# Gate, queries and keys in pairs of column tiles with seven products, and other work beside the values, in a hybrid mLSTM and attention block

## The chip, the cores and the metric

The kernel runs on one core of one Trainium2 chip. The metric is device time in microseconds (us) of one launch, the median of several runs. Everything is computed in fp32; a product of fp32 matrices is made of three TensorE passes over two-part operands (a rounded high part and the rest).

## The reference

One encoder block over 2048 tokens of width 1024. The change is in the first projection and what reads it:

```python
xn = rms_norm(x, g)                         # 2048 x 1024
proj = xn @ W_in                            # q | k | v | o | gates | c_q | c_kv | k_rope
qk = silu(dwconv3_centred(concat([q_pre, k_pre]), conv_w, conv_b))
h = h_fwd + h_bwd                           # chunkwise mLSTM, both directions, 4 heads x 128
y_A = sigmoid(o_pre) * rms_norm(h, norm_g)
q = rms_norm(c_q, q_norm_g) @ w_uq          # 4 heads x (128 + 64), the 64 with rope
kv = rms_norm(c_kv, kv_norm_g) @ w_ukv
h = x + concat([y_A, attention(q, kv, k_rope)]) @ W_out
```

After it come a gated MLP with a convolution and a per-layer input embedding, which the change leaves alone.

## The kernel before

The first projection (`in_proj`) holds all of x in SBUF as two-part operands: `xh[c][f]` and `xl[c][f]` for token quarter c (512 tokens) and half f of the 1024 inputs. It runs in four stages, each of which is a stream of matmuls on PE (the engine of matmuls; DVE, ACT and POOL are the vector, scalar and GpSimd engines, SP issues all DMAs). Each stage is long, and PE's order is that of the code.

The rest stage makes 464 columns (gates, latent queries and keys) for 16 token tiles. A tile of x comes turned from memory (512 KB, in pieces of 512 bytes), ACT casts its high part and DVE subtracts for the low one. Beside it `ssq_x` squares the tile on ACT, adds the eight blocks down to two on DVE (L232, L233) and lets PE sum over the partitions with matmuls against ones (`ssp`, L236); the reciprocal norm goes into `rcol`, and at the end into memory (`r_d`, L319, one DMA of 4-byte pieces).

The values (`OFF_V`, L324) and the output gate (`OFF_O`, L335) follow with 16 tiles of 24 matmuls each, 128 tokens by 512 columns; the mLSTM's gates, a generator, are computed a little at a time beside them. Then queries and keys: eight column tiles j of 128 columns by four token quarters c, transposed, each `block` of 24 matmuls, followed by the convolution over tokens (`conv`: ACT for the first tap, DVE for two more, silu on ACT). Between the matmuls a `pump` (L371) draws 0.986 steps of side work for each six matmuls. The side work is two generators: `absorb` multiplies parts of attention's weights into each other, head by head from `w_out` (`wor`, `woa`, `woo`), and `q_up` makes attention's queries in eight cycles of 256 tokens: load `qraw`, split it (`cq`), multiply, rotate on DVE (`qtt`, `qro`, `qsr`, L598 to L605), transpose, and write to `q_d`.

PE's order in this last stage is written out by hand; the other engines' rows follow from a scheduler that puts an instruction where it thinks it will be ready. Every engine works through its rows in order, SP its DMA issues too: a row that waits holds up all rows behind it on that engine. Working places are named: `x0` to `x15`, `w0` to `w13`, `t0` to `t7`, `u0` to `u2`; who takes a place waits until its last user is done.

The seven-product form exists already in the later MLP (`L1427`): a product of 2 x 2 blocks made of seven block products, with sums of blocks ahead of them and behind. A product there is 12 matmuls of 128 by 512.

Of the kernel before, what the change touches and what calls it, by code (L numbers as in the profile page):

```python
# [19 lines left out]
P = 128  # L20
# [40 lines left out]
class Block:  # L61
# [4 lines left out]
    def __init__(self, ctx, tc, d):  # L66
# [17 lines left out]
        self.o_d = dt([NT, P, 512], F32, name="o_d")  # L84
# [89 lines left out]

    def in_proj(self):
        nc, d = self.nc, self.d
        xh = [[self.at(f"x{4 * c + 2 * f}", [P, 4, 512], F32R, f"xh{c}{f}") for f in range(2)] for c in range(4)]
        xl = [[self.at(f"x{4 * c + 2 * f + 1}", [P, 4, 512], F32R, f"xl{c}{f}") for f in range(2)] for c in range(4)]
        wrot, rrot, trot, srot = _rot("w", (*range(9), 13)), _rot("w", range(9, 13)), _rot("t", range(4)), _rot("s", range(3))
        w_in = d["w_in"][0].rearrange("(a b p) c -> a p b c", b=2, p=P)  # L180

        def load_w(c0, n, before=None):
# [18 lines left out]
            for k2 in range(KT // 2):  # L201
                if k2 == len(raws):
                    load(k2)
                raw = raws[k2]
                for b in range(2):
                    w = self.at(next(wrot), [P, 2, 512], F32R, "wsp")
# [4 lines left out]
        def nat(st, ws, n):  # L211
            ps = self.bank()
            c, o = st // 4, (st % 4) * P
            for kt in range(KT):
                f, k = divmod(kt, 4)
                self.mm3(ps[:, :n], xh[c][f][:, k, o:o + P], xl[c][f][:, k, o:o + P],
                         ws[kt][:, 0, :n], ws[kt][:, 1, :n], kt == 0, kt == KT - 1)
            return ps
# [8 lines left out]
        def ssq_x(st, x_t):  # L227
# [5 lines left out]
            nc.vector.tensor_tensor(ss[:, 0:2], ss[:, 0:2], ss[:, 2:4], op=ALU.add)  # L233
            ps = self.pml.tile([P, 4], F32, name="ssp", tag="ml")
            for i in range(2):
                nc.tensor.matmul(ps, ss[:, i], ones, start=i == 0, stop=i == 1)  # L236
            t = self.stat(1, "rsm")
            nc.vector.tensor_scalar(t, ps[:, 0:1], 1.0 / D, EPS, op0=ALU.mult, op1=ALU.add)
            nc.gpsimd.tensor_tensor(rcol[:, st:st + 1], t, self.nhalf[:, :1], op=ALU.pow)
# [48 lines left out]
        ones = self.cst.tile([P, 4], F32, name="ones")  # L288
        nc.vector.memset(ones, 1.0)
        nq, xq = {}, {}  # L290
# [10 lines left out]
        ws = load_w(OFF_R, NREST, first)  # L301
        for st in range(NT + LAG_X):
            if st + 1 < NT:
                xq[st + 1] = load_x(st + 1)
            if st == 0:
# [4 lines left out]
            if 1 <= st < NT:  # L310
                split_x(st, xq[st])
            if 0 <= st - 1 < NT:
                ssq_x(st - 1, xq.pop(st - 1))
# [6 lines left out]
        gates = self.gates()  # L320

        ws = load_w(OFF_V, 512)
        for st in range(NT):
            ps = nat(st, ws, 512)  # L324
            if st < LAG_R:
                turn_rest(NT - LAG_R + st, nq.pop(NT - LAG_R + st))
            t = self.at(next(trot), [P, 512], name="vo")
            nc.vector.tensor_scalar(t, ps, rcol[:, st:st + 1], None, op0=ALU.mult)
            nc.sync.dma_start(self.v_d[st], t)
            if st >= LAG_R:  # L330
                next(gates, None)

        ws = load_w(OFF_O, 512)
        go = self.row_bcast(self.at("t6", [P, 512], name="go"), d["mlstm_norm_g"][0], 512)
        for st in range(NT):  # L335
            ps = nat(st, ws, 512)
            t = self.at(next(trot), [P, 512], name="vo")
            nc.scalar.activation(t, ps, AF.Sigmoid, scale=rcol[:, st:st + 1])
            nc.vector.tensor_tensor(t, t, go, op=ALU.mult)
            nc.sync.dma_start(self.o_d[st], t)  # L340
            next(gates, None)
        for _ in gates:
            pass

        cw = self.at("w13", [32, P], name="cw")
        nc.sync.dma_start(cw[0:24], d["conv_qk_w"][0].rearrange("t (j p) -> (t j) p", p=P))
        nc.sync.dma_start(cw[24:32], d["conv_qk_b"][0].rearrange("(j p) -> j p", p=P))
        pc = self.tbank([P, 32])
        nc.tensor.transpose(pc, cw, self.ident[:32, :32])
        cwt = self.cst.tile([P, 4, 8], F32, name="cwt")  # L350
        nc.vector.tensor_copy(cwt.rearrange("p a b -> p (a b)"), pc)
        H = S // 2
        side = chain(self.absorb(), self.q_up())
        urot, wrot = _rot("u", (0, 1, 2)), _rot("w", (6, 9, 10, 11))

        def load_qk(j):
            raw = self.at("w12", [P, KT, P], name="wraw")
            nc.sync.dma_start(raw, d["w_in"][0, :, j * P:(j + 1) * P].rearrange("(k p) c -> p k c", p=P))
            out = []
            for f in range(2):  # L360
                w = self.at(next(wrot), [P, 4, 2, P], F32R, "wqk")
# [1578 lines left out]
```

## Time and profile before

| | us |
|---|---|
| median of 3 runs | 2960.42 (2960.11 to 2964.19) |
| profiled execution, span | 2960.1 |
| PE busy | 2893.7 |
| DVE busy | 1991.1 |
| ACT busy | 1477.1 |
| DMA, share of 16 engines | 52.1% |

The median is of whole runs, and the span is that of the profiled execution from its first to its last instruction. Busy time is what an engine spent in its own instructions; a window is a stretch of the span, for which the same is counted. "Idle before, releaser" names what ended an engine's wait. A matmul's own duration in the lists is longer than its pace, since matmuls are pipelined; the pace is the distance between starts.

### The profile page before, as it was taken

What the parts mean: (1) busy time and instruction counts of PE and PEld (TensorE: products, weight loads), DVE (VectorE), ACT (ScalarE), POOL (GpSimd) and SP (SyncE); (2) the same over time, 40 slices, a digit from 0 to 9 for tenths busy, and PEclk for the clock granted to TensorE, in tenths of its full rate; (3) what the DMA queues carried; (4) which work ended last, traced back from release to release, by engine and by line L of the source; (5) the groups of instructions that cost most, each with busy time, mean ns of one, the idle gap of its engine ahead of it and who ended that gap; (6) DMA issues with size and microseconds to landing.
All of it is one profiled execution on the core that took longest, in us unless ns stands there. A gap on an engine that the chain in (4) does not pass through costs nothing.

```text
span 2960.1 us, 40997 instructions
## 1 busy us (share of the span) xinstructions
PE 2893.7 (98%) x14750; PEld 2436.9 (82%) x14750; DVE 1991.1 (67%) x3679; ACT 1477.1 (50%) x2887; POOL 146.5 (5%) x279
## 2 busy tenths in 40 slices
PE   8999999999999999999999999999999999999998
PEld 7888888888888888788788888788887788878776
DVE  7522555777777777635677877767777767676776
ACT  7311544656665666523455555655556333244754
POOL 3100000000000000000000000000000000001111
PEclk9999999999999999999999999999999999999999
DMA  6512444443333343457734544657776657575854
GB/s 193 121 61 92 146 132 153 121 144 99 103 99 101 97 121 114 145 179 262 237 136 168 191 165 152 207 175 236 231 235 194 225 189 241 168 252 197 286 190 157
DMA packets 396540, 496.93 MB, mean 168 GB/s; under 512 B 32416, under 2 KB 265904, under 8 KB 396336
## 3 DMA queue, kind: packets, MB, share of 16 engines
q1 hardware_dynamic: 396336, 494.31, 52.1%
q8 instruction: 116, 1.90, 0.3%
q14 instruction: 88, 0.72, 0.1%
HBM read 318.39 MB, written 175.83 MB: 167 GB/s over the span
## 4 chain that ended last, share of the span: by engine, by line
PE 46%; DVE 4%; DMA 4%; issue 2%; ACT 2%; POOL 0%; SPq 0%; POOLq 0%; ACTq 0%; DVEq 0%
PE fxy L1427 29%; PE fz L1427 12%; PE bk L131 4%; PE fs L131 1%; DMA opr<-t_d 1%; DMA opr<-tw_d 1%; DVE op L121 1%; DVE fw L121 1%; DMA tsum<-x_d 0%; ACT fw L118 0%; DVE pj L1773 0%; ACT junk L1787 0%; DMA h_d<-fh 0%; ACT op L118 0%; PE tb L1075 0%
## 5 line engine op out<-in xcount | busy, mean ns | idle before, releaser
L1427 PE MATMUL fxy<-op,fw 128*128 128x512 f32 x3552 | 854.4, 392 | 18.1 <-DVE fh L1413 5.8
L1427 PEld LDWEIGHTS fxy<-op,fw 128*128 128x128 f32 x3552 | 660.7, 188 | 175.9 <-ACT ug L1584 13.9
L1427 PE MATMUL fz<-op,fw 128*128 128x512 f32 x1776 | 441.0, 391 | 6.5 <-DVE xt L1143 3.3
L1427 PEld LDWEIGHTS fz<-op,fw 128*128 128x128 f32 x1776 | 332.6, 188 | 76.1 <-DVE xt L1143 3.6
L118 ACT CAST pt<-tb 128x512 fp32r<-128x512 f32 x256 | 147.2, 586 | 176.7 <-PE tb L972 176.0
L131 PE MATMUL bk<-wsp,xh 128*128 128x512 f32 (+1 forms) x768 | 234.0, 385 | 0.0
L914 DVE TENSOR_REDUCE mx<-bk 128x1 f32<-128x512 f32 x256 | 175.0, 685 | 69.9 <-PE bk L913 65.1
L1427 PE MATMUL fxy<-op,fwd 128*128 128x512 f32 (+1 forms) x888 | 214.4, 390 | 0.9 <-ACT gate L1768 0.8
L131 PE MATMUL ppv<-pt,kv 128*128 128x256 f32 x1536 | 203.9, 287 | 0.0
L121 DVE TENSOR_TENSOR pt<-tb,pt 128x512 fp32r<-128x512 f32 x256 | 174.0, 684 | 37.5 <-ACT pt L118 36.5
L1427 PEld LDWEIGHTS fxy<-op,fwd 128*128 128x128 f32 x888 | 165.7, 188 | 35.9 <-ACT gate L1768 1.2
L932 ACT ACTIVATE pe<-bk,nm 128x512 f32<-128x512 f32 x256 | 174.6, 696 | 31.3 <-DVE nm L926 27.1
L131 PEld LDWEIGHTS ppv<-pt,kv 128*128 128x128 f32 x1536 | 188.9, 191 | 0.5 <-ACT pt L118 0.4
L131 PE MATMUL bk<-wo,yhl 128*128 128x512 f32 x744 | 176.2, 395 | 5.5 <-DVE yhl L121 5.5
L131 PEld LDWEIGHTS bk<-wo,yhl 128*128 128x128 f32 x744 | 139.3, 189 | 34.4 <-DVE yhl L121 6.0
L131 PEld LDWEIGHTS bk<-wsp,xh 128*128 128x128 f32 x768 | 145.0, 189 | 25.2
L131 PE MATMUL bk<-wsp,xl 128*128 128x512 f32 (+1 forms) x384 | 150.5, 392 | 7.8 <-DVE xl L121 7.8
L131 PE MATMUL bk<-xh,wqk 128*128 128x512 f32 x480 | 157.4, 393 | 0.0
L972 PE MATMUL tb<-ident,pe 128*128 128x128 f32 x1024 | 150.2, 273 | 3.2 <-DVE pt L121 3.2
L972 PEld LDWEIGHTS tb<-ident,pe 128*128 128x128 f32 x1024 | 122.3, 141 | 22.0 <-DVE pt L121 4.6
L118 ACT CAST fw<-hraw 128x1024 fp32r<-128x1024 f32 (+1 forms) x72 | 70.2, 981 | 125.2 <-PE fxy L1427 96.2
L1413 DVE TENSOR_TENSOR fh<-fh,fxy 128x512 f32<-128x512 f32 x95 | 65.1, 685 | 94.6 <-PE fxy L1427 94.2
(359 smaller groups left out, 4852.2 us busy)
## 6 DMA issues: line engine op xcount, KB each, us to landing
fwr<-in_w_up SPq DMA_DIRECT2D x66, 512.0 KB, 4.4
fh<-h_d SPq DMA_DIRECT2D x48, 512.0 KB, 4.0
h_d<-fh SPq DMA_DIRECT2D x48, 512.0 KB, 4.0
s_d<-fwr SPq DMA_DIRECT2D x44, 512.0 KB, 2.6
fws<-s_d SPq DMA_DIRECT2D x44, 512.0 KB, 3.7
rw<-row_d SPq DMA_DIRECT2D x32, 512.0 KB, 4.7
tw_d<-tsum SPq DMA_DIRECT2D x60, 256.0 KB, 5.0
opr<-tw_d SPq DMA_DIRECT2D x60, 256.0 KB, 5.4
```

The costliest lines, as they stand in the source:

```text
L118: nc.scalar.copy(hi, src)
L121: (sub or nc.vector).tensor_tensor(lo, src, _f(hi), op=ALU.subtract)
L131: mm = lambda *a, **k: self.nc.tensor.matmul(*a, **k, skip_group_check=more)
L914: nc.vector.tensor_reduce(s.mx[:, kb:kb + 1], ps, axis=AX.X, op=ALU.max)
L932: nc.scalar.activation(s.pe[:, kb % 2], s.banks[kb], AF.Exp, bias=s.nm, scale=ASCALE, accum_out=s.rs[:, kb:kb + 1])
L972: nc.tensor.transpose(t[:, j, :], s.p[kb][:, j * P:(j + 1) * P], self.ident)
L1413: add = lambda o, a, b: tt(o, a, b, op=ALU.add)
L1427: nc.tensor.matmul(out, a[:, k * P:(k + 1) * P], parts[lo][:, cols], start=first, stop=lo == 1 and k == last, skip_group_check=more)
```

## The change

The output gate, the queries and the keys are no longer made tile by tile. Their 12 column tiles are taken as six pairs, each for the high 1024 tokens first and then for the low ones: 12 pairs of seven products. The weights (with the norm's gain) are scaled on ACT and written to memory as column tiles (`wg_d`), and read again for each pair; sums of their blocks are made on DVE (`in_prep`). The operands from x are sums of blocks too: those of the high tokens are made from reloaded x (`highs`) and split into the places of old ones; those of the low tokens are scaled by the reciprocal norm, summed (`lows`) and written to memory (`xn_d`), and come back when the pairs turn to the low half (`load`).

The values now run with these generators, the gates, `absorb` and `q_up` drawn beside each three matmuls (`beside`, `VRATE` 1.15), and in another order of token tiles (0 to 7, 12 to 15, 8 to 11). The sums of squares come from x in its own layout (a second load of each tile, `x_r`) by ACT's accumulator. The mLSTM's norm gain moves into the output projection's weights (`gmix`), and the gate is multiplied in after the transpose of h. The convolutions that were left for the attention stage go.

```diff
-            sq = self.at("w13", [P, KT, P], name="x_sq")
-            nc.scalar.activation(sq, x_t, AF.Square)
-            ss = self.at("t7", [P, 4, P], name="x_ss")
-            nc.vector.tensor_tensor(ss, sq[:, 0:4], sq[:, 4:8], op=ALU.add)
-            nc.vector.tensor_tensor(ss[:, 0:2], ss[:, 0:2], ss[:, 2:4], op=ALU.add)
...
+            nc.scalar.activation(self.at("t7", [P, D], BF16, "junk"), x_r, AF.Square, accum_out=ss)
+            self.rsq(ss, 1, 1.0 / D, rcol[:, st:st + 1])
...
+        def wgs():
+            def scale(i, t):
+                for k in range(4):
+                    kt = 4 * (i % 2) + k
+                    nc.scalar.activation(t[:, k], t[:, k], AF.Copy, scale=gcol[:, kt:kt + 1])
+                    nc.sync.dma_start(self.wg_d[4 * (i // 2):4 * (i // 2) + 4, :, kt, :].rearrange("c p e -> p c e"),
+                                      t[:, k].rearrange("p (c e) -> p c e", e=P))
...
+        def lows():
+            rl = self.row_bcast(self.at("u2", [P, H], name="rrl"), self.r_d[0:H], H)
...
+                for f in range(2):
+                    tt(t[:, f], t[:, f], rl, op=ALU.mult)
+                b11, t1, b21, b22 = t[:, 0, :SB], t[:, 0, SB:], t[:, 1, :SB], t[:, 1, SB:]
...
+                tt(t1, t1, b11, op=ALU.subtract)
+                tt(t2, b22, t1, op=ALU.subtract)
+                yield
+                tt(t3, t2, b11, op=ALU.subtract)
+                tt(t4, b21, t2, op=ALU.subtract)
+                for i, o in enumerate((b11, t1, t2, b21, t3, t4, b22)):
+                    nc.sync.dma_start(self.xn_d[i, :, k], o)
...
+        def beside():
+            n = when[0]
+            when[0] += 1
...
+            if n >= 4:
+                when[1] += self.VRATE
+                while when[1] >= 1:
+                    if next(side, self) is self:
+                        when[2] = True
+                    when[1] -= 1
+            if n >= 33 and n % 3 == 0:
+                next(scaled, None)
+            if n >= 62 and n % 2 == 0:
+                next(turned, None)
+            if n >= 68 and n % 2 == 1 and (n < 82 or when[2]):
+                next(raised, None)
...
+    def prod(self, out, w, ops, more=False, cols=slice(0, SB)):
+        wh, wl = w
+        first, last = not more, len(ops) - 1
+        for a, lo in ((wh, 0), (wl, 0), (wh, 1)):
+            for k, parts in enumerate(ops):
+                self.nc.tensor.matmul(out, a[:, k * P:(k + 1) * P], parts[lo][:, cols], start=first,
+                                      stop=lo == 1 and k == last, skip_group_check=more)
+                first = False
...
-                nc.vector.scalar_tensor_tensor(hh[:, h, :], hh[:, h, :], r4[:, h:h + 1], og[:, h * P:(h + 1) * P],
-                                               op0=ALU.mult, op1=ALU.mult)
+                nc.vector.tensor_scalar(hh[:, h, :], hh[:, h, :], r4[:, h:h + 1], None, op0=ALU.mult)
...
-            nc.scalar.copy(hy[:, 1], pt)
+            nc.vector.tensor_tensor(hy[:, 1], pt, og, op=ALU.mult)
```

Three places show how this moves rows. On DVE, one cycle of query up before: the rotation's six instructions (`qtt`, `qro`), then the weights of the next column tile (`wqk`).

```order
L598 TENSOR_TENSOR qtt<-qpr,qcs 128x128
L599 TENSOR_TENSOR qtt<-qpr,qcs 128x128
L600 TENSOR_TENSOR qtt<-qpr,qcs 128x128
L601 TENSOR_TENSOR qtt<-qpr,qcs 128x128
L602 TENSOR_TENSOR qro<-qtt 128x4x32
L603 TENSOR_TENSOR qro<-qtt 128x4x32
L127 SCALAR_TENSOR_TENSOR wqk<-wraw,gcol,wqk 128x128 x2
L605 TENSOR_TENSOR qsr<-qro,qsr 128x4x64
L121 TENSOR_TENSOR cq<-qraw,cq 128x512
```

And the end of cycle 4 and the start of cycle 5 in the change: between them stand the first sums of the low tokens (`xs`, `xsum`), which wait for the reciprocal norms as a row (`rrl`) and for reloaded x.

```order
L804 TENSOR_TENSOR qtt<-qpr,qcs 128x256
L805 TENSOR_TENSOR qroom<-qtt 128x8x32
L807 TENSOR_TENSOR qroom<-qroom 128x8x64
L375 TENSOR_TENSOR xs<-xs,rrl 128x1024
L378 TENSOR_TENSOR xs<-xs 128x512
L375 TENSOR_TENSOR xs<-xs,rrl 128x1024
L379 TENSOR_TENSOR xsum<-xs 128x512
L381 TENSOR_TENSOR xsum<-xsum,xs 128x512
L382 TENSOR_TENSOR xsum<-xs,xsum 128x512
L800 TENSOR_TENSOR qtt<-qpr,qcs 128x256
L801 TENSOR_TENSOR qtt<-qpr,qcs 128x256
L802 TENSOR_TENSOR qroom<-qtt 128x8x32
```

What moved: query up's rotation, once followed by weights that were long loaded, now stands behind sums of data that is loaded in the same stage. On SP, the end of a cycle of query up before, between the convolution's writes (`qk_d`):

```order
L623 DMA q_d<-qo 128x4x256
L568 DMA qraw<-rest_d 128x2x256
L414 DMA qk_d<-ct 128x4x128
L622 DMA q_d<-qso 128x4x128
L414 DMA qk_d<-ct 128x4x128
L358 DMA wraw<-in_w_in 128x8x128
L622 DMA q_d<-qso 128x4x128
```

And in the change, where the loads for these sums are issued:

```order
L465 DMA v_d<-vo 128x512
L817 DMA q_d<-qo 128x4x256
L147 DMA rrl<-r_d 128x1024
L358 DMA xs<-in_x_turned 128x1024 x2
L775 DMA qraw<-rest_d 128x2x256
L787 DMA qcs<-in_rope 128x2x64
L825 DMA q_d<-qso 128x4x128
L384 DMA xn_d<-xs 128x512
L358 DMA xs<-in_x_turned 128x1024
L825 DMA q_d<-qso 128x4x128
```

What moved: query up's loads and results now share the queue with the token loads, the sums' writes (`xn_d`) and, just ahead, the scaled weights (`wg_d`). On PE, parts of two blocks of that stage before, with query up (`qpr`) between its matmuls:

```order
L131 MATMUL bk<-xl_128,wqk 128x512
L131 MATMUL bk<-xh_120,wqk 128x512 x2
L131 MATMUL bk<-xl_128,wqk 128x512
L131 MATMUL bk<-xh_120,wqk 128x512
L131 MATMUL qpr<-wq,cq 128x256 x6
L131 MATMUL bk<-xh_121,wqk 128x512
L131 MATMUL bk<-xl_129,wqk 128x512
L131 MATMUL bk<-xh_121,wqk 128x512 x2
```

And the first pair after the values in the change (`fw` and `op` are the pair's weights and operands; each product is 12 matmuls):

```order
L517 MATMUL bk<-xh_122,fw_2785 128x512 x8
L517 MATMUL bk<-xl_130,fw_2785 128x512 x4
L517 MATMUL tb<-op,fw_2793 128x512 x4
L517 MATMUL tb<-op,fw_2794 128x512 x4
L517 MATMUL tb<-op,fw_2793 128x512 x4
L517 MATMUL bk<-op,fw_2799 128x512 x12
L517 MATMUL bk<-xh_123,fw_2785 128x512 x8
L517 MATMUL bk<-xl_131,fw_2785 128x512 x4
L517 MATMUL bk<-op,fw_2793 128x512 x4
L517 MATMUL bk<-op,fw_2794 128x512 x4
```

What moved: the queries' stage is now products without side work between them, and query up stands among the values' matmuls instead.

More of the change, by code (lines that the diff above doesn't have):

```diff
@@ L353, in in_proj @@
+        gates, scaled, turned, raised = self.gates(), wgs(), lows(), highs()
         side = chain(self.absorb(), self.q_up())
[L354 to L361, printed above, removed]
-                for k in range(4):
-                    kt = 4 * f + k
-                    self.split_g(raw[:, kt], gcol[:, kt:kt + 1], w[:, k, 0], w[:, k, 1])
-                out.append(w)
-            return out
@@ L539, in absorb @@
         for h in range(NH):
[L540 removed]
+            wh, wl = [self.at(t, [P, D], F32R, "woa") for t in ("w12", "w13")]
             self.split(raw, wh, wl)
@@ L1419, in up_down, with prod @@
             pass
-        def prod(out, w, x, more=False, cols=slice(0, SB)):
-            wh, wl = w
-            ops = self.xop[x]
-            first, last = not more, len(ops) - 1
-            for a, lo in ((wh, 0), (wl, 0), (wh, 1)):
-                for k, parts in enumerate(ops):
-                    nc.tensor.matmul(out, a[:, k * P:(k + 1) * P], parts[lo][:, cols], start=first,
-                                     stop=lo == 1 and k == last, skip_group_check=more)
-                    first = False
+        def prod(out, w, x, *a):
+            self.prod(out, w, self.xop[x], *a)
         def rest_y(s):
```

523 lines of the change are left out of this document (340 added, 183 removed).

## The prediction

> **What bounds the kernel now.** I read the page first, then busy time by stages, then the chain of waits. The page's busy row, and seven stages of the answer by windows (start and end, length, then busy us of PE, PEld, DVE, ACT, POOL, granted clock, DMA share, GB/s):
>
> ```profile
> PE 2893.7 (98%) x14750; PEld 2436.9 (82%) x14750; DVE 1991.1 (67%) x3679; ACT 1477.1 (50%) x2887; POOL 146.5 (5%) x279
> 7.60:109.60 102.00, 99.77 (x517) 88.06 (x518) 73.45 (x263) 68.97 (x151) 36.09 (x61) 1.00 0.69 166
> 109.60:197.00 87.40, 87.40 (x395) 71.93 (x395) 31.75 (x93) 10.23 (x26) 1.14 (x3) 1.00 0.26 88
> 197.00:283.30 86.30, 86.30 (x382) 71.47 (x381) 12.77 (x23) 12.78 (x20) 0.00 (x0) 1.00 0.16 59
> 283.30:512.80 229.50, 229.37 (x1182) 194.81 (x1181) 129.93 (x327) 108.78 (x209) 0.00 (x0) 1.00 0.50 153
> 512.80:540.00 27.20, 23.21 (x130) 19.90 (x129) 18.58 (x39) 20.91 (x39) 0.00 (x0) 0.87 0.31 97
> 540.00:1210.00 670.00, 660.18 (x4483) 593.61 (x4482) 491.19 (x1279) 406.42 (x1113) 44.81 (x62) 1.00 0.35 109
> 1210.00:1460.00 250.00, 238.37 (x1189) 198.75 (x1188) 134.90 (x203) 92.86 (x166) 14.49 (x34) 0.99 0.68 222
> ```
>
> In order these are the rest columns, the values, the output gate, queries and keys, the seam to attention, attention, and the output projection. The first four are bound by PE: it idles 2.2 us in the first and 0.13 us in the next three together. So a matmul removed there is time gained, as long as PE stays fed. The second thing to see is the DMA share: 0.26 and 0.16 beside the values and the gate. The changed kernel puts its new traffic exactly there.
>
> The price of a 128x512 matmul is in the chain of waits, in the stage that already works with seven products (start, us, what):
>
> ```profile
> 1474.26 5.44 PE fxy L1427 x24
> ```
>
> 24 in 5.44 us is 0.2267 us each. The values' 384 then make 87.05 us, the length of their stage.
>
> **What goes.** (1) Gate, queries and keys were 384 + 768 = 1152 matmuls; twelve pairs of seven products of 12 are 1008. 144 × 0.2267 = **−32.6 us**. (2) The sums of squares leave PE. Four `ssp` matmuls and their neighbours in the timeline of the rest stage, then PE's waits there:
>
> ```profile
> 59.76 0.51 PE L236 MATMUL ssp<-ones,x_ss 128*128 128x4 f32 x4
> 60.13 0.45 PE L131 MATMUL bk<-wsp,xl 128*128 128x464 f32 x1
> PE ssp L236 <- DVE x_ss L233: 2.0, 3, 0.9
> ```
>
> From start to start the four take 0.37 us, sixteen times 5.9; with the 2.0 of waits **−7.9 us**. ACT squares as before and adds an accumulator read, under a PE that is busy 99.77 of 102 us while ACT has 33 us free; if that cover went, 16 reads cost about 3 us. Together −40.5 us.
>
> **What moves into the values.** The side work (absorb and query up) leaves the queries' stage. Its size there is 229.37, less 765 matmuls of queries and keys × 0.2267 = 173.4 and 20 score matmuls = 4.5: 51.5 us. Free-running, the new values' stage is 87.05 + 51.5 = 138.5 us. That alone gains and loses nothing; the question is whether everything that is fed into these 138.5 us arrives. Three things don't, by my count.
>
> First, absorb. It has one raw buffer for four heads; before, its loads, casts and sums stand so in the tile's own answer:
>
> ```profile
> L118 ACT CAST woa<-wor x4: 1035/1042/1053, 284.1 to 315.3; 128x1024 fp32r<-128x1024 f32 x4
> L121 DVE TENSOR_TENSOR woa<-wor,woa x4: 1215/1226/1226, 285.2 to 316.4; 128x1024 fp32r<-128x1024 f32 x4
> DMA to landing us min/median/max: 3.6/3.6/3.6
> ```
>
> A load can only be issued when the split has read the buffer: 3.6 + 1.04 + 1.23 + about 0.3 to issue = 6.2 us per head. Side work is now drawn 1.15 times per 3 matmuls (0.986 per 6 before), so PE asks for a head every 2.6 steps × 0.68 + 6 × 0.2267 = 3.1 us. Three heads at 3.1 short: 9 us.
>
> Second, traffic. Between the first scaled-weight load (its place is free at step 28 of 128, when the last matmul of tiles 0 to 3 with the first half of x is through) and the last high-token load, SP issues 12.6 MB of weights out and back, 15.7 MB of token loads and sums, 9.6 MB of query up and 3.4 MB of values: 41.3 MB. PE needs 105 us for the same stretch. What the DMA engines can move, from two windows of the trace (DMA busy tenths in 40 slices, then GB/s), first 7.6 to 109 us, where 512-byte pieces of x go, and then 1240 to 1252 us with larger ones:
>
> ```profile
> DMA  9999971658657478627059653544755625639999
> GB/s 368 283 283 295 273 213 29 194 167 251 180 149 194 143 210 234 189 74 204 0 158 287 170 168 68 202 113 104 245 147 181 162 104 135 221 9 44 27 17 115
> ```
> ```profile
> DMA  9999999999989640172520267999999998866567
> GB/s 382 423 410 423 396 437 410 369 389 362 326 289 284 171 121 23 32 213 67 156 55 0 84 162 224 305 312 343 406 347 362 336 362 335 328 253 253 219 166 263
> ```
>
> Full engines give 283 GB/s with the small pieces and about 380 with the large. The scaled weights are written back in 512-byte pieces, as half of query up's results are: 10.2 MB / 283 + 31.1 / 380 = 118 us even if no load ever waits for an instruction.
>
> The Trainium skill ("DMA: Bandwidth & Descriptors", Specifications) gives 512 bytes as enough for line rate and about 358 GB/s as a core's limit to HBM; by that the 41.3 MB are an estimated 115 us. The trace disagrees on both: 283 at 512 bytes, slices above 400 with larger pieces.
>
> Third, order. DVE and SP work in order, and the sums of the low tokens stand on DVE between query up's instructions (shown with the change). Taking absorb's 9, step 28 comes 41 us into the stage (28 × 0.68 = 19, plus 13 for the 24 of some 90 draws of side work, plus 9). The first sums need about 21 MB through SP first: at 320 GB/s, between the two rates, 66 us, so 107. Six sums (DVE 1.23 for 1024 columns, 0.684 for 512) take 5.2, and cycle 5 of query up, due at 97 with absorb's 9 in it, is queued behind them. The last cycle's rotation stands behind the sums of the third high load, some 16 MB further on: 45 us at 350, so its transposes come at about 152 instead of 110, and 42 bare steps × 0.68 = 28.6 remain. The stage ends at 181, not 138.5: **+43 us**. Ends: 9, if the traffic hides; 62, if all of it goes at 283 (41 + 37.2 / 0.283 + 28.6 = 201). I take 43, nearer to the mixed rate that the two rows give.
>
> **What else.** The reciprocal norms are written to memory in 4-byte pieces, now ahead of the values' weight loads on SP. In the old run that write and what followed it look so (window 96 to 109):
>
> ```profile
> 96.00:109.00 13.00, 13.00 (x67) 11.45 (x66) 7.25 (x28) 8.12 (x20) 2.84 (x7) 1.00 1.05 42
> ```
>
> Engines full at 42 GB/s for some 10 us, hidden since the weights were mostly ahead of it. Now the values' first weights come behind: 0 to 8 us, I take 2, since 13 us lay between the write and the start of the values. The 16 new row loads of x (8.4 MB) meet a stage at share 0.69, saturated in its first 13 us: 0 to 5, I take 1.
>
> In the pairs PE needs 84 × 0.2267 = 19.04 us each. DVE's prices are in these rows of the two existing stages:
>
> ```profile
> L121 DVE TENSOR_TENSOR fw<-fwr,fw 128x1024 fp32r<-128x1024 f32 x88 | 107.3, 1220 | 31.2 <-ACT fw L118 31.2
> L1413 DVE TENSOR_TENSOR fh<-fh,fxy 128x512 f32<-128x512 f32 x95 | 65.1, 685 | 94.6 <-PE fxy L1427 94.2
> L1471 DVE SCALAR_TENSOR_TENSOR fgv<-uv,fcw,fgv 128x1024 f32<-128x1024 f32 x88 | 112.7, 1281 | 11.2 <-ACT fgv L1469 10.5
> ```
>
> A high query pair has 3 splits of 1220, 5 operations on operands and 6 on results of 685 and 4 taps of 1281: 16.3, with small ones 17 of 19.04; gate pairs 11.8, low ones less. Where the pairs turn from high to low tokens, 28 operand splits (19.2 us) fall into two pairs: 24.9 and 21.7 against 19.04, a backlog of 8.5 of which 5.4 is slack in PSUM. I take **+3** (0 to 8).
>
> The seam loses its convolutions of the last tile. Its 27.20 us hold 4.0 of idle PE and a half-clock stretch:
>
> ```profile
> 521.91 0.68 PE L762 MATMUL mb<-v,kk 128*128 128x129 f32 x4 [2.16 <-issue]
> 523.96 1.23 PE L762 MATMUL mb<-v,kk 128*128 128x129 f32 x4 [1.36 <-DVE cb L766]
> 527.12 0.63 PE L909 MATMUL bk<-kv,q_s 128*128 128x512 f32 x1
> 527.54 0.63 PE L910 MATMUL bk<-kr,q_t 128*128 128x512 f32 x1
> ```
>
> Matmuls 0.42 apart instead of 0.2267, after 3.5 us of idling almost in one piece. Less waits there: **−4** (−8 to 0). The same behaviour charges long waits inside the values: +1 (0 to 5). In attention PE is busy 660 of 670 us, and what the change moves from ACT to DVE (16 products of 0.69) lies under it; the gains in the output projection's splits lie under 238 us of PE. Both at 0; without cover 5.
>
> The Trainium skill ("TensorE: Matmul & The Clock Gate", Part 1) says the rate halves after an idle window of about 3.4 us and recovers after as long a busy one; the 3.5 us above agree.
>
> **The sum.** −40.5 + 43 + 2 + 1 + 3 − 4 + 1 = +5.5 us. The profiled execution has a span of 2960.1, a fraction of a us under the median of 2960.42: forecast **2966 us**, own range 2950 to 2978.
>
> **Rivals.** *The traffic hides.* Loads run ahead of their use, and larger pieces go at 380 or more. The values then lose 9 to 22 (118 − 105 + 9); −40.5 + 9 to 22 + 3 gives 2932 to 2945. For it: PE is the only engine with a handwritten order, the others' follows readiness; against it: 41.3 MB in 105 us asks for 393 GB/s, which no window above holds for 10 us. *The skill's line rate* ends in the same place: 115 − 105 + 9 = 19, 2942. *SP as the bound (slower).* SP's writes of query up's results wait for ACT, and token loads stand behind them; each such wait empties the queue, and all goes at 283: the stage ends at 201, and −40.5 + 62 + 3 gives 2985. It decides once the average falls under 310 GB/s. *DVE falls behind where the pairs change half*, with the full 8.5 and again in the next pairs: +10 on the forecast, 2976.
>
> **Chances.** Forecast 0.45 (0.10 of it faster, 0.17 same, 0.18 slower); traffic hidden 0.30; SP bound 0.17; DVE 0.08. Faster by over 0.2% (6 us, about what a measurement tells from no change) 0.40, within 0.17, slower 0.43. The range 2930 to 2986 leaves out 2 in 10. Both signs hold much, so the forecast's own range stands above.
>
> **What would show it.** The windows: a rest stage of about 94 us; a values' stage near 181 with DMA share above 0.85 and PE idle some 43, ended by DVE or DMA; twelve pairs in about 230. In the waits, PE's transposes of query up behind DVE behind `xs` loads. It is wrong if the values' stage is near 140 to 160, or the share there stays under 0.8 while PE waits.

## The result and the profile after

The changed kernel takes 3010.1 us (median of 4 runs, 3003.93 to 3014.07) beside 2961.7 of the kernel before: 1.0158 times as long (95% interval 1.0144 to 1.0173), 48 us slower. The profiled execution has a span of 3008.5, against 2960.1.

The change's stages in the new run, by windows (start and end, length, busy PE, PEld, DVE, ACT, POOL, granted clock, DMA share, GB/s):

```profile
7.69:101.97 94.28, 91.32 (x436) 80.21 (x436) 49.96 (x193) 63.37 (x151) 28.84 (x74) 0.98 0.78 229
101.97:113.84 11.87, 0.00 (x1) 0.01 (x1) 1.10 (x2) 1.80 (x3) 0.00 (x0) 0.64 0.83 142
113.84:320.90 207.06, 158.50 (x800) 131.07 (x801) 104.31 (x228) 86.50 (x153) 2.53 (x6) 0.89 0.84 268
320.90:566.70 245.80, 239.37 (x1044) 196.85 (x1043) 177.19 (x276) 147.91 (x192) 0.00 (x0) 0.99 0.48 145
```

These are the rest stage, a gap in which PE does nothing, the values with the side work, and the pairs. The account against the run before, up to the first twelve matmuls of the output projection (PE, `wo` from `wo` and `yhl`; 1233.30 before, 1272.80 after, +39.5):

| | before | after | predicted | measured |
|---|---|---|---|---|
| rest stage, to its end | 109.6 | 101.97 | −7.9 + 1 | −7.6 |
| gap ahead of the values | 0 | 11.87 | +2 | +11.9 |
| values with side work | 87.05 + 51.5 = 138.5 | 207.06 | +43 + 1 | +68.6 |
| from there to the output projection | 984.8 | 951.9 | −32.6 + 3 − 4 | −32.9 |
| the rest of the kernel | 1726.8 | 1735.7 | 0 | +8.9 |

The fourth row before is 1233.30 − 197.00, less the 51.5 of side work. The last row is no effect of its own that I could find: the code there is the same in the changed kernel and in all experiments, and it took between 1725 and 1737 us in the profiles of the experiments. So the gain came in the size that was forecast (its parts did not, see below), and two terms lost about twice what it brought.

The gap in the timeline of the new run (start, us, engine, line, what, then the wait ahead and what ended it), first on SP, the norms' write and the values' weights:

```profile
96.68 0.38 SPq L327 DMA_DIRECT2D r_d<-rcol  x1
97.10 0.93 SPq L199 DMA_DIRECT2D wraw<-in_w_in  x1
100.67 13.88 SPq L199 DMA_DIRECT2D wraw<-in_w_in  x2
```
Then on ACT, the next two rows after the rest stage's last:

```profile
111.98 1.33 ACT L128 ACTIVATE wsp<-wraw,gcol 128x512 fp32r<-128x512 f32 x2 [13.91 <-DMA wraw<-in_w_in]
113.22 0.56 ACT L290 COPY rt<-rtp 128x512 f32<-128x512 f32 x1
```
And on PE, the first row after 101.97:

```profile
113.84 1.12 PE L288 MATMUL rtp<-ident,nn 128*128 128x128 f32 x4 [11.87 <-ACT rt L290]
```

The write of the reciprocal norms is issued at 96.68 and the values' first weights right behind it. They reach ACT only at 111.98, after 13.91 us; behind ACT's scaling stands the copy `rt` of the rest stage's last transposes, and PE's next row waits for that copy. The write has landed after 12.9 us, and SP itself stood at the issue of two further weight loads until 114.6.

The values' stage cut where its traffic changes: at the first load of weights to be scaled, at the first sum of the low tokens, and at query up's last transposes.

```profile
113.84:166.70 52.86, 40.80 (x168) 30.02 (x169) 26.77 (x83) 24.08 (x47) 2.53 (x6) 0.89 0.57 178
166.70:236.80 70.10, 53.02 (x308) 46.01 (x307) 21.06 (x56) 34.03 (x60) 0.00 (x0) 0.89 0.99 305
236.80:288.60 51.80, 32.41 (x191) 28.25 (x190) 40.68 (x66) 16.24 (x28) 0.00 (x0) 0.86 1.00 330
288.60:320.90 32.30, 32.27 (x137) 26.78 (x138) 15.81 (x26) 12.14 (x18) 0.00 (x0) 0.93 0.72 235
```

The reader is to see the DMA shares 0.99 and 1.00 of the second and third row: for 122 us the engines had no free time. Together they moved this (window 178 to 300):

```profile
DMA packets 36831, 38.65 MB, mean 317 GB/s; under 512 B 3345, under 2 KB 27665, under 8 KB 36823
...
q1 hardware_dynamic: 36823, 38.55, 98.6%
```

38.65 MB in 122 us. PE's waits in the stage (line waited at, what ended the waits, us in total, times, longest):

```profile
PE gb L822 <- DVE qroom L807: 32.7, 5, 10.7
...
PE gps L934 <- ACT qso L824: 3.2, 1, 3.2
PE gb L739 <- DMA ukvt<-in_w_ukv_turned: 3.0, 1, 3.0
PE gb L133 <- DVE woa L123: 2.9, 4, 0.9
PE gb L133 <- ACT woa L120: 2.7, 3, 1.1
PE qpr L133 <- DVE cq L123: 2.4, 1, 2.4
```

32.7 us are query up's transposes waiting for the rotation on DVE. The prediction named this wait, but its reason, sums of the low tokens ahead of the rotation, holds for a part only. The first two of the five (9.0 us at 217 and 4.2 us at 234) come before the first of these sums, which starts at 236.8. There DVE waited for query up's own rows of cosines and sines (`qcs`), in DVE's timeline:

```profile
212.49 0.42 DVE L800 TENSOR_TENSOR qtt<-qpr,qcs 128x256 f32<-128x256 f32 x1 [15.05 <-DMA qcs<-in_rope]
229.79 0.42 DVE L800 TENSOR_TENSOR qtt<-qpr,qcs 128x256 f32<-128x256 f32 x1 [12.63 <-DMA qcs<-in_rope]
```

SP issued these two loads at 205.2 and 226.0, behind loads and writes of the scaled weights. The other three waits (1.0, 7.7 and 10.7 us) come after the sums have begun. PE is busy for 158.5 us where the free-running sum is 138.5; the granted clock of 0.89 (at most 207 × 0.11 = 23 us lost) is enough to account for that difference.

### The profile page after: what moved, and what is told of

Its sections match the earlier page's. It is cut to its first block, busy times and chain, and to the rows that moved or that the text cites. A ratio compares the mean times of both kernels' runs of the same rounds, so it can differ in the third digit from the quotient of the medians.

```text
span 3008.5 us, 40779 instructions
## 1 busy us (share of the span) xinstructions
PE 2880.1 (96%) x14542; PEld 2417.0 (80%) x14542; DVE 2078.5 (69%) x3678; ACT 1561.5 (52%) x2955; POOL 137.7 (5%) x295
## 3 DMA queue, kind: packets, MB, share of 16 engines
q8 instruction: 114, 1.87, 0.3%
## 4 chain that ended last, share of the span: by engine, by line
PE 72%; DVE 9%; DMA 8%; ACT 5%; issue 4%; POOL 1%; SPq 1%; ACTq 0%; POOLq 0%; DVEq 0%
PE fxy L517 28%; PE fz L517 11%; PE bk L133 6%; PE ppv L133 5%; PE bk L517 4%; PE tb L1174 3%; PE tb L517 2%; PE bk L1111 2%; PE bk L1113 2%; PE bk L1115 2%; PE bk L1112 2%; PE bk L1114 2%; PE fs L133 1%; DMA opr<-tw_d 1%; DVE op L123 1%
## 5 line engine op out<-in xcount | busy, mean ns | idle before, releaser
L517 PE MATMUL fxy<-op,fw 128*128 128x512 f32 x3552 | 857.5, 393 | 18.4 <-DVE fh L1618 6.3
L133 PE MATMUL bk<-wsp,xh 128*128 128x464 f32 (+1 forms) x512 | 163.5, 402 | 0.2 <-DVE wsp L129 0.2
L123 DVE TENSOR_TENSOR fw<-fwr,fw 128x1024 fp32r<-128x1024 f32 x88 | 107.4, 1220 | 30.7 <-ACT fw L120 30.7
L120 ACT CAST op<-opr 128x512 fp32r<-128x512 f32 x165 | 95.7, 618 | 51.1 <-PE fxy L517 20.0
L1669 DVE SCALAR_TENSOR_TENSOR fgv<-uv,fcw,fgv 128x1024 f32<-128x1024 f32 x88 | 112.8, 1281 | 10.6 <-ACT fgv L1667 9.9
```

The lines of the kernel that those rows point to most:

```text
L120: nc.scalar.copy(hi, src)
L123: (sub or nc.vector).tensor_tensor(lo, src, _f(hi), op=ALU.subtract)
L133: mm = lambda *a, **k: self.nc.tensor.matmul(*a, **k, skip_group_check=more)
L517: self.nc.tensor.matmul(out, a[:, k * P:(k + 1) * P], parts[lo][:, cols], start=first, stop=lo == 1 and k == last, skip_group_check=more)
L1669: nc.vector.scalar_tensor_tensor(t, u[:, tap:tap + 2 * SB], taps[:, tap, ct:ct + 1], t, op0=ALU.mult, op1=ALU.add)
```

## The experiments

All kernels are the changed one with the edit named. The table has the time and its ratio to the kernel before, and from each profile the values' stage: its start, its length, how long PE was idle in it, and the DMA share; then when the output projection's first block begins, which leaves out the variation behind it.

| run | us | ratio (95%) | start | length | idle | DMA | to output projection |
|---|---|---|---|---|---|---|---|
| changed kernel | 3010.1 | 1.0158 (1.0144 to 1.0173) | 113.8 | 207.1 | 48.6 | 0.84 | 1272.8 |
| e1_r_rows | 2993.1 | 1.0100 (1.0083 to 1.0117) | 105.9 | 207.1 | 49.6 | 0.82 | 1261.5 |
| e2_scale_in_pairs | 2974.9 | 1.0047 (1.0032 to 1.0063) | 114.4 | 180.8 | 23.5 | 0.73 | 1245.9 |
| e3_no_lows | 2982.8 | 1.0073 (1.0058 to 1.0088) | 113.9 | 187.6 | 31.8 | 0.75 | 1252.5 |
| e5_lows_on_pool | 3007.5 | 1.0152 (1.0132 to 1.0172) | 113.2 | 212.8 | 50.9 | 0.81 | 1276.5 |
| e4_absorb_two | 3004.9 | 1.0143 (1.0128 to 1.0158) | 111.8 | 205.8 | 47.5 | 0.83 | 1268.6 |
| e6_rate | 2999.4 | 1.0129 (1.0113 to 1.0145) | 115.1 | 202.9 | 47.4 | 0.85 | 1268.7 |
| e8_large_pieces | 3002.5 | 1.0138 (1.0124 to 1.0153) | 114.5 | 205.8 | 47.7 | 0.82 | 1271.1 |
| c1_rows_scale | 2965.5 | 1.0016 (1.0006 to 1.0025) | 105.6 | 176.8 | 28.0 | 0.74 | 1233.3 |
| c2_rows_scale_absorb | 2963.3 | 1.0005 (0.9995 to 1.0015) | 106.1 | 177.4 | 25.4 | 0.73 | 1233.0 |
| c3_rate | 2955.8 | 0.9988 (0.9978 to 0.9998) | 106.3 | 169.9 | 21.4 | 0.76 | 1224.0 |
| c4_early | 2955.4 | 0.9980 (0.9970 to 0.9990) | 106.6 | 170.1 | 18.4 | 0.76 | 1228.6 |
| f1_rate_no_lows | 2944.9 | 0.9944 (0.9929 to 0.9959) | 104.1 | 161.0 | 11.3 | 0.58 | 1214.1 |
| f2_splits_on_pool | 2963.1 | 1.0006 (0.9997 to 1.0014) | 106.4 | 170.2 | 20.2 | 0.76 | 1231.9 |

The start is that of the rest stage's transposes right ahead of the values' first matmul; in c1, c2 and f2 it is half a us later, at the transpose of the norms behind them.

**e1_r_rows**, the norms turned before they are written:

```diff
-        nc.sync.dma_start(self.r_d.rearrange("(t p) -> p t", p=P), rcol)
+        pr = self.tbank([P, P])
+        nc.tensor.transpose(pr[:NT, :], rcol, self.ident)
+        rrt = self.at("t6", [P, P], name="rrt")
+        nc.vector.tensor_copy(rrt[:NT, :], pr[:NT, :])
+        nc.sync.dma_start(self.r_d.rearrange("(t p) -> t p", p=P), rrt[:NT, :])
```

> The reciprocal norms are turned by PE and written as 16 rows of 512 bytes instead of 2048 pieces of 4 bytes. Late start theory: the 11.9 us in which PE stands still ahead of the values (102.0 to 113.8) and the 13.7 us at half clock behind them (6.8 us lost) both come from the piecewise write that stands ahead of the values' weights: 3008.5 falls to about 2990 (17 to 19 us less). Rival, that the weights are late for want of a free place: the wait stays above 8 us and the time falls by 4 us at most.

17 us less, as the theory had it, but not in the places it named. The write is now issued behind the values' weights and after their stage has begun (first row, SP), and a wait of 2.4 us is left of the 11.9 (second row, PE):

```profile
111.84 0.34 SPq L331 DMA_DIRECT2D r_d<-rrt  x1
105.89 0.66 PE L288 MATMUL rtp<-ident,nn 128*128 128x128 f32 x4 [2.38 <-ACT rt L290]
```

The stage starts 8 us sooner and is as long as before, 207.1 us, although the half clock at its start is gone: its first part isn't set by PE's rate. (Of the 13.7 us at half clock in the changed kernel 8.5 lay in the wait itself, where PE did nothing; so 2.6 us at most were to be had there, not 6.8.) The other 9 us of the median lie behind the stage, 3 ahead of the output projection and the rest in the part that varies from run to run; that the total came out as said is luck. So the write, as it stood ahead of the weights, accounts for 8 us of the gap. Whether its 2048 pieces or its place did it isn't separated: the edit changes both.

**e2_scale_in_pairs**, no scaled weights in memory:

```diff
-            self.nc.sync.dma_start(t, self.wg_d[c])
+            o = (0, OFF_O, OFF_K)[c // 4] + c % 4 * P
+            self.nc.sync.dma_start(t, self.d["w_in"][0, :, o:o + P].rearrange("(k p) c -> p k c", p=P))
...
+        for t in self.raw[i]:
+            for k in range(KT):
+                nc.scalar.activation(t[:, k], t[:, k], AF.Copy, scale=self.gcol[:, k:k + 1])
```

> The scaled weights are not written and read back: each pair loads its two column tiles from the weights themselves and ACT scales them there (16 instructions of 128x128 per pair). 12.6 MB less beside the values, the same bytes in the pairs. Traffic theory (the values' stage moves 55.5 MB at a full rate of 320 GB/s and lasts as long as that): the stage shortens by 35 to 40 us, the whole by 30 to 40, to about 2972. Order theory (the waits come from query up standing behind the sums on DVE, whatever the traffic): 10 us less at most. ACT in a pair goes from about 11 to 17 us of 19; if that is too much, the pairs grow by 5 us or more.

35 us less, of which 26 in the values' stage and nothing given back in the pairs, which took 243.7 us from their first matmul to the last (243.1 before the edit). 12.6 MB for 26 us would be 480 GB/s, above the 317 of the full stretch, so not all of these bytes had set the stage's length. PE's wait for the rotation, 32.7 us in five pieces before, is now in the list of waits:

```profile
PE gb L827 <- DVE qroom L812: 10.2, 4, 4.4
```

10.2 us in four, none above 4.4, and all four come after the first sum of the low tokens (195.6 here). The two waits for `qcs` ahead of it are gone, and the later ones are shorter although the sums stand on DVE as before. So the weights' trip through memory delayed both. Whether it did so by its bytes or by its place ahead of `qcs` on SP isn't shown.

**e3_no_lows** leaves out the low tokens' sums (their loads, 24 operations on DVE and their writes).

```diff
-        gates, scaled, turned, raised = self.gates(), wgs(), lows(), highs()
+        gates, scaled, turned, raised = self.gates(), wgs(), iter(()), highs()
...
-                nc.sync.dma_start(raw, self.xn_d[list(self.INX).index(name), :, k])
+                nc.sync.dma_start(raw, self.d["x_turned"][:, k, 0:SB])
```

> The sums of the low tokens are left out, with their loads and writes (11.5 MB) and 20.7 us of DVE; the pairs of the low tokens load x itself in the same pieces. Traffic theory: 36 us less in the values' stage. Order theory: the 32.7 us in which PE's transposes wait for DVE go, and some 12 us of half clock with them: 40 us less. Neither, if the absorb stage and the scaled weights set the end: under 15 us less.

27 us less, 19.5 in the stage: less than either theory said. The wait for the rotation is 15.2, all of it in the two cycles that wait for `qcs` (9.9 and 5.3 us), and 11.3 ahead of the values remain.

**e5_lows_on_pool** was to tell the two apart, since it takes the sums off DVE and keeps the bytes:

```diff
-                    tt(t[:, f], t[:, f], rl, op=ALU.mult)
+                    nc.gpsimd.tensor_tensor(t[:, f], t[:, f], rl, op=ALU.mult)
...
-                tt(t1, t1, b11, op=ALU.subtract)
+                gt(t1, t1, b11, op=ALU.subtract)
```

> The same sums on GpSimd instead of DVE, all traffic kept. Order theory (query up's rotation waits because it stands behind the sums on DVE): its waits go and the whole falls by 20 us or more. Traffic theory: the data is late in any case, the whole changes by 6 us at most, or grows if GpSimd is slow.

No change in the time, and a stage 5.7 us longer. GpSimd needs 2.64 us for what DVE does in 1.22. But DVE had no less to do: it was busy for 103.3 us of the stage, 104.3 before the edit and 84.4 in e3, since its own instructions took longer beside GpSimd. Between 225 and 300 us, eight of its splits of 128x512 that ran beside GpSimd's sums for nine tenths of their time or more took 1.87 us in the mean, and eight that ran without them 0.69. Query up's waits are still 32.1 us. Of these, 8.2 and 4.5 come before the first sum, for `qcs` as before; so these two have nothing to do with where the sums stand. For the later waits this run doesn't tell late bytes from the order on DVE; that e2 shortens them with the order kept speaks for the bytes.

**e4_absorb_two** and **e6_rate** change what PE and its side work ask for, and no bytes:

```diff
-            r = self.at("w11", [P, D], name="wor")
+            r = self.at(("w11", "u2")[h % 2], [P, D], name="wor")
```

> Only the raw rows of the absorb stage alternate between two places, so that a head's load is issued ahead of the split before it. Absorb's waits in the changed kernel are 5.6 us at its matmuls and some of the clock loss behind them. If the values' stage is set by its own waits one after another: 6 to 9 us less, about 3002. Traffic theory: the full DMA engines from about 178 to 300 us set the end and these start when the fourth tile is through, so what absorb gains comes through only as far as it brings that start forward: 0 to 6 us less.

```diff
-    VRATE = 1.15
+    VRATE = 0.95
```

> Only the rate of the side work is lowered, 1.15 to 0.95, in the changed kernel itself. Traffic theory: the engines are full from 178 to 300 us and set when the last cycle can go; but 18 bare steps (12 us) that stood behind it now stand ahead, so 5 to 12 us less. If the order of PE alone set the stage, nothing changes (within 4 us).

The first gains 5 us, 1.3 of it in the stage and 2 in its start; the second 11 us, 4.1 in the stage, where the longest wait for the rotation is now one cycle earlier. Neither goes beyond what the traffic theory allows.

**e8_large_pieces** writes the scaled weights as they stand in the tile:

```diff
-                    nc.sync.dma_start(self.wg_d[4 * (i // 2):4 * (i // 2) + 4, :, kt, :].rearrange("c p e -> p c e"),
-                                      t[:, k].rearrange("p (c e) -> p c e", e=P))
+                    nc.sync.dma_start(self.wg_d[i // 2, :, kt, :], t[:, k])
...
-            self.nc.sync.dma_start(t, self.wg_d[c])
+            self.nc.sync.dma_start(t, self.wg_d[c // 4, :, :, c % 4 * P:c % 4 * P + P])
```

> The scaled weights are written in pieces of 2 KB instead of 512 bytes, and read back in pieces of 512 bytes in the pairs, where the engines are half idle. If small pieces cost the full engines what the two windows of the prediction say (283 against 380 GB/s), 6.3 MB go through 5.7 us sooner: 4 to 7 us less. If 512 bytes already go at line rate: within 3 us.

From the first weight load to the first sum it takes 67.7 us instead of 70.1, and the stage is 1.3 us shorter. The median is 7.6 us lower, but the intervals of the two ratios overlap. This is inconclusive for the time; in that stretch the small pieces cost some 2 us, less than the 5.7 that the two windows of the prediction gave. The run also bears on a rival that the prediction did not name, SP's own issuing: SP took 0.87 us in the median to issue one of these 24 writes, and 0.47 in e8. That the stretch is hardly shorter speaks against SP's issuing as its bound.

**c1_rows_scale** puts e1 and e2 together.

> Norm rows turned by PE and weights scaled in the pairs, together. If the two causes are separate, their gains add: 3010.1 - 17.0 - 35.2 gives 2958 (2954 to 2962). If the late start only hid part of the traffic, the sum is larger than either but stays above 2966.

2965.5, nearly 8 us over the sum of the two. At the output projection they do add: 11.3 and 26.9 us less make 38.2, and it begins 39.5 us sooner, exactly where it began before the change. Two causes, then, give back the whole loss up to there.

**c2_rows_scale_absorb** and **c3_rate** add absorb's second place, and then the lower rate, to c1.

> As the run before with absorb's two raw places. With the traffic down to 43 MB the engines are no longer full, so absorb's waits (about 7 us in the run with weights scaled in the pairs, and a stretch of half clock after them) should come through: 7 to 12 us less than the run before, 2946 to 2951. Rival: the token loads still set the end, within 4 us of it.

> As the run before, with the side work drawn 0.95 times instead of 1.15 times per three matmuls, so that it ends at step 104 instead of 86 of 128 and fewer bare matmuls are left behind the last cycle of query up. If query up waits for data that comes at its own time, 18 steps of 0.68 us move under the wait: 5 to 12 us less, about 2940. If the stage is bound by PE by then, within 4 us of the run before.

The second place gains nothing that can be told (2.2 us, the stage unchanged). Absorb's waits do fall, from 11.9 us to 6.6, but the rotation's stay at 11.3, and PE is busy for 152.0 us instead of 148.8 at a granted clock of 0.94 instead of 0.97. The time is the rival's; that the token loads set the end isn't shown. The lower rate then gains 7.5 us in the time and about as much in the stage. With it the kernel is as fast as the one before, or by the interval a little faster.

**c4_early** starts the low tokens' loads sooner, in c3:

```diff
-                t = self.at(("x11", "x1")[k % 2], [P, 2, H], name="xs")
+                t = self.at(("x11", "x12")[k % 2], [P, 2, H], name="xs")
...
-            if n >= 62 and n % 2 == 0:
+            if n >= 34 and n % 4 == 2:
                 next(turned, None)
```

> As the run with the lower rate of side work, and with the low tokens' loads and sums begun at step 34 instead of 62, one piece per four steps instead of two, in two places that the missing weight traffic leaves free. The same bytes, begun earlier. Traffic theory (engines full only from about step 60 on, and query up's last cycles behind them): the 9.8 us wait of the last cycle and most of the half clock go, 10 to 20 us less, 2936 to 2946, faster than the kernel before by 0.5% or more. Rival, that query up waits for the rotation's place among the sums on DVE wherever they stand: the waits move to earlier cycles and the time stays within 5 us of 2956.

The expectation of 10 to 20 us fell, and the rival's time came out. The long wait of 9.7 us became three of up to 3.8, one of them behind a wait of DVE for `qcs` (3.2 us) (PE's waits in c4's stage):

```profile
PE gb L831 <- DVE qroom L816: 9.8, 3, 3.8
PE gb L748 <- DMA ukvt<-in_w_ukv_turned: 3.3, 1, 3.3
PE rtp L288 <- ACT rt L290: 2.8, 1, 2.8
PE gps L902 <- DVE mg L898: 2.4, 1, 2.4
PE gb L133 <- DVE woa L123: 2.0, 3, 0.8
```
And the DMA engines are full somewhat earlier (windows of 20 us):

```profile
166.00:186.00 20.00, 19.02 (x117) 16.36 (x115) 16.16 (x29) 6.28 (x11) 0.00 (x0) 1.00 0.84 270
186.00:206.00 20.00, 16.75 (x92) 14.72 (x93) 15.29 (x26) 7.78 (x13) 0.00 (x0) 0.91 1.01 331
206.00:226.00 20.00, 16.30 (x88) 14.14 (x87) 10.05 (x19) 6.10 (x11) 0.00 (x0) 0.83 1.02 336
226.00:246.00 20.00, 17.79 (x111) 15.66 (x110) 13.76 (x28) 9.91 (x17) 0.00 (x0) 1.00 0.69 220
```

From 186 to 226 the share is 1.01 and 1.02; in c3 it is 0.95, 0.99 and 0.88 in the three windows from 190 to 250. c4 is 0.2% ahead of the kernel before; it can't be told from c3, and these two are the fastest that compute everything.

**f1_rate_no_lows** is c3 with e3's edit, and leaves out the same sums.

> As the run with the lower rate of side work (norm rows turned, weights scaled in the pairs, two raw places, 0.95), and the sums of the low tokens left out with their 11.5 MB; the low pairs load x itself. It asks whether traffic still accounts for the 30 us by which the values' stage there (169 us) exceeds its free-running 138.5. Traffic theory: the engines are no longer full for long, and the stage falls to 150 us or less, the whole by 18 us or more. Rival, that the dense side work (waits of transposes for rotations, half clock after them) costs as much by itself: the stage stays above 160 us.

11 us less, and a stage of 161.0, a hair above the rival's bound. The engines are at 0.58 in the mean here:

```profile
106.90:126.00 19.10, 15.27 (x64) 12.39 (x64) 7.14 (x25) 7.61 (x16) 1.13 (x3) 0.80 0.75 227
126.00:146.00 20.00, 16.45 (x69) 11.70 (x68) 14.41 (x40) 11.16 (x20) 0.00 (x0) 0.98 0.62 217
...
206.00:226.00 20.00, 16.77 (x93) 14.32 (x92) 8.85 (x18) 8.96 (x17) 0.00 (x0) 0.91 0.48 150
```

PE idles 11.3 us and is busy for 149.8, 11 over the free-running sum, at a granted clock of 0.80 to 0.98 in its first 40 us and 0.91 around a wait of 3.2 at 210. So without this traffic some 22 us of the loss remain, half in short waits (3.5 us for absorb's `ukvt`, 3.2 for a rotation, 2.3 for the gates and smaller ones) and half in PE being busy for longer. The half clock, 17 us of it in this stage, explains at most 8.5 of that half.

**f2_splits_on_pool** is c4 with half of the low operands' splits on GpSimd.

> As the run with the early low sums, and half of the 28 splits of the low tokens' operands have their subtraction on GpSimd instead of DVE. Every run so far has a 4.5 us wait of PE for DVE where the pairs change from high to low tokens, with a stretch of half clock. DVE theory (the splits fall into two pairs that need 25 and 22 us of DVE in 19): 9.6 us less on DVE there, the wait goes, 4 to 7 us less. Rival, GpSimd is so much slower (1.47 us for 128x512 in the run with the sums there, against 0.68) that the operands come later: the wait stays or grows.

The wait where the pairs change half grew from 4.5 to 5.4 us and a second of 2.3 came; GpSimd takes 1.75 us for what DVE does in 0.68, and DVE's own splits beside it took up to 1.78. The kernel is 7.7 us slower than c4, with intervals apart. The rival holds, and what would remove that wait stays open.

## Why the prediction was wrong, point by point

**What goes.** Right in its sums, in part by luck. The rest stage ends 7.6 us sooner (−7.9 and +1 said), and from the end of the values to the output projection 32.9 us are gained (−32.6 + 3 − 4 said). But these 32.9 are not where they were forecast. By windows, first the seam and attention before, then the pairs and the seam and attention after:

```profile
512.80:1233.30 720.50, 706.69 (x4776) 634.69 (x4775) 525.70 (x1363) 441.87 (x1190) 44.81 (x62) 1.00 0.35 108
320.90:563.96 243.06, 236.63 (x1030) 194.55 (x1028) 175.53 (x273) 145.22 (x189) 0.00 (x0) 0.99 0.48 146
563.96:1272.80 708.84, 701.73 (x4762) 631.51 (x4761) 528.00 (x1368) 427.26 (x1160) 44.85 (x64) 1.00 0.37 111
```

Gate, queries and keys took 86.3 + 229.5 − 51.5 = 264.3 us of their own before and take 243.1 as pairs: 21.2 gained, where −32.6 + 3 was said. The seam and attention take 11.7 us less, where 4 was said; 6.7 of that is PE's idle time. One miss of 8.4 us and one of 7.7 cancel. The pairs do pay where they change half, as forecast; PE's waits there in the new run:

```profile
PE bk L517 <- DVE uv L652: 4.5, 1, 4.5
PE tb L517 <- DVE fw L123: 1.9, 2, 1.1
```

Together 6.4 us, where I had taken 3 of 0 to 8, and 6.8 us at half clock behind them, which I had not counted.

**The late start** was mis-sized, +2 for +11.9. The bounds of 0 to 8 were wrong: I set the 10 us of crawling engines against the 13 us between the write and the values' start, and left out what stands behind the late load on ACT. The values' weights are scaled by ACT, the copy of the last transposes stands behind that in ACT's order, and PE needs the copy before its first matmul of the stage. e1 shows the write, as it stood ahead of the weights, as the cause of the wait.

**The values' stage** is the term that took the time out of the range: +43 for +68.6, each of its four parts too short in the same direction.

| part | predicted | measured |
|---|---|---|
| to the first load of scaled weights | 41 | 52.9 |
| to the first sum of low tokens | 66 | 70.1 |
| to the last transposes of query up | 45 | 51.8 |
| bare steps | 28.6 | 32.3 |

The frame was right: full DMA engines and PE behind DVE's rotation, with 0.99 and 1.00 of share where I had said above 0.85 for the stage, and rates nearly as said (305 and 330 GB/s for 320 and 350). The step "Third, order" was wrong in part: it put the rotation behind the sums of the low tokens, and 13.2 of its 32.7 us come before any sum, while it waits for `qcs` behind the scaled weights. e3, without the sums, keeps these two waits (15.2 us); e2, without the weights' trip, loses them.

In the sum, PE's idle time is nearly right: 48.6 us, some 43 said. The term that failed most is the clock, "+1 (0 to 5)": PE is busy for 20 us more than the free-running sum, and 46 us of the stage are granted half. That is no cost of its own where PE waits for data anyhow: in e1 the stage kept its length without the half clock at its start. The first part shows both, 12 us late before most of that traffic: PE is idle 12.1 (9 said for absorb; absorb's waits are 8.6, of which 3.0 for `ukvt`, and query up's first split adds 2.4) and busy 40.8 for 32, with 11.9 us at half clock.

The rival with the hidden traffic is refuted by the DMA shares and by e2. The rival "SP as the bound" came nearest in size (2985; 201 for the stage, 207 measured), but its mechanism, queues emptied by SP's waits for ACT, isn't what the shares show: the queues were full. The rule of the Trainium skill ("DMA: Bandwidth & Descriptors", Specifications) of about 358 GB/s to a core gave 2942 and doesn't hold as the rate to plan with here: 317 GB/s is what 122 us at a share of 0.986 moved.

**Which cause how much.** Turning the norms' write, which also puts it behind the weights, and taking away the weights' trip through memory bring the output projection's start back to 1233.3, its place before the change. What remains against the 33 + 8 us of gain is then in the values' stage: 38 us above 138.5 in c1, 31 in c3, 22 in f1. The step from c3 to f1, 9 us, is the low sums' traffic and DVE time together; the 22 left weren't taken apart further.

**The last row of the account** (+8.9 behind the output projection) had no term. Kernels with the same code there differ by nearly as much, so part of it is chance; how much isn't settled.

## What to carry to other kernels

Before work is moved beside a stage, add up the bytes that the stage will have to move and divide by what full DMA engines moved over a long stretch in the same kernel, not by the best slice; if that comes near the stage's length, the traffic will not hide. Look at every load that a step needs, the small ones too: 64 KB of `qcs` behind the scaled weights held up the rotation twice. A write in 4-byte pieces doesn't belong ahead of the loads that the next stage starts with (e1 turned it and put it behind them at once); follow what stands behind the late load on each engine to its end. And a gain measured at the end can be checked at a landmark in the middle, where parts add that don't seem to at the end; but look at its parts too, since a sum that fits can hold two misses.

## What the runs showed of the hardware that was not expected

A write of 8 KB in 2048 pieces took 12.9 us to land, and ACT waited 13.9 us for the load issued right behind it. GpSimd took 2.64 us for a 128x1024 product and 1.47 to 1.75 for a 128x512 sum, about twice of DVE's 1.22 and 0.68; and DVE's own splits of 0.69 us took 1.87 beside it (e5). Starting the same traffic 28 steps earlier (c4) changed nothing, and writing in larger pieces (e8) gained 2.4 us in the stretch where the weights went.

The clock fell to half after short waits too. Four windows of 3.4 us in the new run's absorb stage:

```profile
136.00:139.40 3.40, 3.24 (x15) 2.27 (x13) 0.87 (x3) 1.50 (x4) 0.00 (x0) 1.00 0.72 251
139.40:142.80 3.40, 1.68 (x6) 1.19 (x7) 1.23 (x1) 1.87 (x3) 0.00 (x0) 1.00 0.48 145
142.80:146.25 3.45, 2.87 (x8) 1.69 (x6) 0.29 (x1) 2.04 (x4) 0.00 (x0) 0.51 0.83 285
146.25:149.60 3.35, 2.54 (x9) 1.61 (x9) 1.22 (x1) 1.16 (x3) 0.00 (x0) 1.00 0.59 153
```

In the second row PE was busy for 1.68 of 3.40 us, and its waits there were 1.12 and 0.76 us, none near 3.4. The third row is granted 0.51. After it, 2.54 busy of 3.35 kept the full clock. The Trainium skill ("TensorE: Matmul & The Clock Gate", Part 1) speaks of an idle window of about 3.4 us; here one that was half idle was enough.

It isn't always. The clock changes on a grid of 3.41 us. On this grid, in nine of the traces (before, the changed kernel, e1, e2, e3, c1, c3, c4, f1), all 85 windows at full clock in which PE was busy for under 40% were followed by half clock, and none of the 7509 in which it was busy for 55% or more. Of the 58 between, 18 were. At half clock all 51 windows under 80% stayed there, and all 82 over 90% went back to full clock.
